# A fused convolution and attention layer: weights loaded from ScalarE's queue, and background work given out by estimated time

## The chip, the core and the metric

The kernel runs on one core of a Trainium2 chip. The time is the device time of one execution in microseconds (us); lower is better. TensorE (PE) multiplies matrices into PSUM, VectorE (DVE), ScalarE (ACT) and GpSimd (POOL) do elementwise work, and SyncE (SP) only issues transfers (DMA) here. Each engine runs its instructions in order and waits on semaphores where one needs another's result.

## The reference

One layer over 2048 positions of width 2048, in float32, cut to its core:

```python
proj = x @ w_in + b_in                                   # 2048 x 5376
c_val, c_glu, c_gate, q, k, v, a_gate = split(proj)
h = c_val * sigmoid(c_glu)                               # 1024 channels
h = causal_depthwise_conv(h, conv_w, 31 taps) + conv_b
y_conv = silu(layer_norm(h)) * silu(c_gate)
# 16 query heads of 64, 2 key/value heads, window 128, a learned sink per head
y_attn = window_attention(q, k, v, sinks) * silu(a_gate)
y = concat(y_conv, y_attn) @ w_out + b_out
out = layer_norm(2 ** 0.25 * x + y)
```

## The kernel before

**Three products for one.** To keep float32 accuracy each operand is split into a high part (rounded to the matmul format `fp32r`, a ScalarE copy, L135) and a low part, the rest (a subtraction, `lo_part`, L138, on VectorE or POOL). `mm3` (L795 to L797) then makes three matmuls of 128x512: high x high, low x high, high x low.

**Steps.** The program is written out as a list of 432 steps, each one weight tile of 128x1024 and 24 matmuls. The first 208 belong to the input projection: four chunks of 512 positions with 52 steps each. In a chunk, 8 steps `first` make four output tiles (k, v and the first convolution pair) side by side, 36 steps `in` make 18 tiles one after the other, and 8 steps `last` make four tiles side by side again. Then come 112 steps `gate` and 112 steps `out`, which use a Strassen scheme: two blocks with seven products each, of sums of weight quarters (`T`, `O` are those sums and their low parts, made by `tsum_part` on POOL and put aside in memory) and of sums of inputs (`gen_y`). Attention blocks (`att_scores`, `att_transpose`, `att_values`, three steps apart) are placed at steps 13 to 41 of each chunk.

**Weights.** At step n the program loads the weight tile of step n+3 (`load_w`), loads the stored low part of step n+2 (`load_lo`) where there is one, and splits step n+2 (`split_w`): a ScalarE copy, and a POOL subtraction where no low part is stored. Low parts of chunk 0 are stored (`wlo`) and loaded again in chunks 1 to 3. There are three buffers each of raw tile, high part and low part, so the load of a low part waits until TensorE has finished step n-1.

**Transfers.** `dma` (L75 to L77) issues everything from SP, in the order of the program: weights, inputs, intermediate results, stores. A transfer that waits for its source or its buffer holds all behind it. `store_later` puts a store a few steps behind the work that makes its source.

**Background work.** VectorE's convolution (31 taps for each 128 channels and chunk, L234 and L237) and the normalizations wait in a queue `tq` and a generator `convs`; `run_bg(n)` takes n items at the end of each step: 4 or 5 in the input steps, 3 or 4 in gate, 1 or 2 in out. Within an engine, the build orders instructions by the program's order and its own simulated readiness.

**The end.** The last four steps run row block by row block, each followed by its normalization (`tail_norm`) and stores; their weights are loaded by `tail_w` into other buffers.

Of the kernel before, what the change touches and what calls it, by code (L numbers as in the profile page):

```python
# [16 lines left out]
P = 128  # L17
# [13 lines left out]
NSLOT = 69  # L31

# [16 lines left out]

@with_exitstack  # L50
def hybrid_layer_kernel(ctx, tc, x, xT, w_first, w_in, w_out, consts, b_out, ln_g, ln_b, out):
    nc = tc.nc
    V, A, G, T = nc.vector, nc.scalar, nc.gpsimd, nc.tensor
# [17 lines left out]
    def dma(out, in_):  # L71

        if queue:
            with tc.issue_after(queue.pop()):
                queue.append(nc.sync.dma_start(out=out, in_=in_).ins)  # L75
        else:
            queue.append(nc.sync.dma_start(out=out, in_=in_).ins)  # L77

# [301 lines left out]
    def evac_in(c, t, kind, j, ps):  # L380
# [11 lines left out]
        elif kind == "k":  # L392
            for t in (*ks, *kl):
                copy(t[:, 0:P], t[:, 4 * P:5 * P].bitcast(F32))
# [15 lines left out]
        elif kind == "v":  # L410
            raw = slot(f"vraw{c}")
            A.activation(out=raw, in_=ps, func=AF.Identity, bias=b1)
            copy(vt[:, 0], vt[:, 4].bitcast(F32))
# [160 lines left out]
    wlo = [dram.tile([P, 1024], F32, tag=f"wlo{n}", name=f"wlo{n}") for n in range(52)]  # L574
# [70 lines left out]
    def out_norm(c):  # L645
# [9 lines left out]
        def fin(n):  # L655
            def f():
                if n + 2 < 16:
                    d, s = units[n + 2]
                    load_z(c, s, d)
                if n < 16:  # L660
                    d, s = units[n]
                    if s == 0 and d < 3:
                        load_gb(c, d + 1)
                    norm_unit(c, s, d)
                if n >= 4:
                    d, s = units[n - 4]
                    store(c, s, d)
            return f
        return [first] + [fin(n) for n in range(20)]
# [35 lines left out]
    def load_w(n, parts=1):  # L705
# [171 lines left out]

    w0 = load_w(0, 2)
# [16 lines left out]
    for n, s in enumerate(steps):  # L895
# [24 lines left out]
        if n < PER:  # L920
# [3 lines left out]
        if s[0] in ("first", "last"):  # L924
# [15 lines left out]
            if p == 7 and s[0] == "first":  # L940
                for t in (2, 3, 1, 0):
# [4 lines left out]
            run_bg(5)  # L946
        elif s[0] == "in":
# [10 lines left out]
            run_bg(4 if 13 <= n % PER < 42 else 5)  # L958
        elif s[0] == "gate":
# [11 lines left out]
            run_bg(3 + n % 2)  # L971
        else:
# [28 lines left out]
            run_bg(2 if blk == 1 and (i == 4 or i == 7 and n % 2) or len(tq) > 20 else 1)  # L1001
# [6 lines left out]
            if n == len(steps) - 1:  # L1008
                run_bg(len(tq))
                tail_banks()  # L1010
                for tp in range(4):
# [3 lines left out]
                    tail_norm(3, tp)  # L1015
        if n < TAIL:
# [9 lines left out]
    run_bg(len(tq))  # L1026
# [67 lines left out]
```

## Time and profile before

| | |
|---|---|
| median of 3 runs | 2646.96 us (2645.77 to 2650.88) |
| the profiled execution | 2649.56 us, span 2647.8 us |
| busy: PE, DVE, ACT, POOL | 96%, 78%, 50%, 38% |
| moved by DMA | 720.43 MB, mean 272 GB/s |
| granted TensorE clock, mean | 0.989 |

The span runs from the first to the last instruction. Engine shares are busy time by span; SP's issues aren't counted as busy. In the rows shown below, a group is written as line, engine, operation, written tile <- read tiles, with its count; a wait as "who <- for whom: us in total, times, longest".

### The profile page before, as it was taken

Reading aid. Unit: us, or ns where it says so; the run is one execution under the profiler, and the core shown is the slowest. Engines: PE = TensorE matmul, PEld = TensorE weight load, DVE = VectorE, ACT = ScalarE, POOL = GpSimd, SP = SyncE. Lnnn points to the kernel's source line nnn. Section 1 sums busy time; section 2 is a strip of 40 time slices with the busy share of each in tenths; the row PEclk is TensorE's granted clock in tenths of the full one; section 3 lists DMA queues with packets and bytes.
Section 4 is the critical chain, followed back from the end, with each engine's and each line's share of the span. In section 5 each row is a group of like instructions: output and inputs, shape, how many; then the busy total and the mean of one; then the engine's idle time right before and its main releaser. Section 6 shows DMA issues by size and latency. Waiting matters only on the chain.

```text
span 2647.8 us, 35533 instructions
## 1 busy us (share of the span) xinstructions
PE 2547.2 (96%) x11680; PEld 2107.5 (80%) x11680; DVE 2069.5 (78%) x3215; ACT 1328.5 (50%) x2520; POOL 1006.3 (38%) x636
## 2 busy tenths in 40 slices
PE   8999999999899999999999999999999999999986
PEld 7788877877688887888887787888888888888875
DVE  3787798868888858889759899987775677987676
ACT  4677335776347765467536434544554323333244
POOL 2777824455144451426423222324222222222246
PEclk9999999999999999999999999999999999999998
DMA  8675898757987689866887667786888987899876
GB/s 282 218 259 198 285 330 272 244 176 267 343 297 246 202 304 348 319 227 224 270 277 250 238 232 270 272 285 217 287 287 289 331 299 281 285 347 351 277 255 244
DMA packets 331674, 720.43 MB, mean 272 GB/s; under 512 B 37856, under 2 KB 95328, under 8 KB 331488
## 3 DMA queue, kind: packets, MB, share of 16 engines
q1 hardware_dynamic: 331488, 718.16, 78.3%
q8 instruction: 92, 1.51, 0.2%
q14 instruction: 94, 0.77, 0.1%
HBM read 564.79 MB, written 153.21 MB: 271 GB/s over the span
## 4 chain that ended last, share of the span: by engine, by line
PE 52%; DVE 22%; DMA 10%; ACT 7%; issue 4%; SPq 2%; POOL 2%; DVEq 0%; ACTq 0%; POOLq 0%
DVE cv L237 7%; PE in L797 4%; PE in L795 4%; PE in L796 4%; PE out L796 3%; PE out L797 3%; PE out L795 3%; SPq L75 2%; PE out_s L796 2%; PE out_s L797 2%; PE out_s L795 2%; PE gate_s L797 1%; PE gate_s L795 1%; PE gate_s L796 1%; ACT pr L325 1%
## 5 line engine op out<-in xcount | busy, mean ns | idle before, releaser
L138 POOL TENSOR_TENSOR wl<-wr,wh 128x1024 fp32r<-128x1024 f32 (+1 forms) x158 | 397.9, 2520 | 938.8 <-ACT wh L135 679.1
L135 ACT ACTIVATE wh<-wr 128x1024 fp32r<-128x1024 f32 (+1 forms) x436 | 455.1, 1046 | 529.1 <-DMA wr<-in_w_in_dram 68.6
L237 DVE SCALAR_TENSOR_TENSOR cv<-h,cst,cv 128x512 f32<-128x512 f32 x928 | 696.4, 752 | 18.8
L795 PE MATMUL in<-xh,wh 128*128 128x512 f32 x1280 | 503.7, 394 | 10.1 <-ACT xh L135 5.8
L797 PE MATMUL in<-xh,wl 128*128 128x512 f32 x1280 | 501.4, 393 | 11.3 <-DMA wl<-wlo 11.2
L796 PE MATMUL in<-xl,wh 128*128 128x512 f32 x1280 | 501.7, 392 | 0.0
L797 PEld LDWEIGHTS in<-xh,wl 128*128 128x128 f32 x1280 | 241.9, 189 | 65.3 <-DMA wl<-wlo 15.3
L795 PEld LDWEIGHTS in<-xh,wh 128*128 128x128 f32 x1280 | 242.2, 189 | 59.9 <-ACT xh L135 6.6
L796 PEld LDWEIGHTS in<-xl,wh 128*128 128x128 f32 x1280 | 242.0, 189 | 48.7 <-DVE xl L138 1.0
L135 ACT ACTIVATE yhout<-yrout 128x512 fp32r<-128x512 f32 x112 | 70.0, 627 | 223.8 <-DVE yrout L560 206.2
L796 PE MATMUL out<-wl,yhout 128*128 128x512 f32 x448 | 174.9, 390 | 5.9 <-POOL wl L138 5.9
L797 PE MATMUL out<-wh,ylout 128*128 128x512 f32 x448 | 174.4, 389 | 0.0
L138 POOL TENSOR_TENSOR plc<-pmc,phc 128x512 fp32r<-128x512 f32 x64 | 83.1, 1299 | 222.4 <-ACT phc L135 194.7
L795 PE MATMUL out<-wh,yhout 128*128 128x512 f32 x448 | 166.5, 389 | 0.0
L138 DVE TENSOR_TENSOR ylgate<-yrgate,yhgate 128x512 fp32r<-128x512 f32 x112 | 110.9, 991 | 42.4 <-ACT yhgate L135 41.1
L138 DVE TENSOR_TENSOR ylout<-yrout,yhout 128x512 fp32r<-128x512 f32 x112 | 103.4, 925 | 50.7 <-ACT yhout L135 49.4
L325 ACT ACTIVATE pr<-pr,sm 128x128 f32<-128x128 f32 x256 | 99.6, 390 | 68.7 <-DVE sm L321 68.3
L135 ACT ACTIVATE yhgate<-yrgate 128x512 fp32r<-128x512 f32 x112 | 69.9, 624 | 114.8 <-DVE yrgate L560 94.3
L795 PE MATMUL gate_s<-yhgate,wh 128*128 128x512 f32 x304 | 118.8, 391 | 2.8 <-DVE g L454 2.6
L797 PE MATMUL gate_s<-yhgate,wl 128*128 128x512 f32 x304 | 118.7, 390 | 2.5 <-POOL wl L138 1.9
L796 PE MATMUL gate_s<-ylgate,wh 128*128 128x512 f32 x304 | 118.3, 389 | 0.0
L795 PE MATMUL gate<-yhgate,wh 128*128 128x512 f32 x288 | 112.7, 391 | 0.2 <-DVE g L454 0.2
(383 smaller groups left out, 5914.3 us busy)
## 6 DMA issues: line engine op xcount, KB each, us to landing
wl<-wlo SPq DMA_DIRECT2D x156, 512.0 KB, 5.3
wr<-in_w_in_dram SPq DMA_DIRECT2D x144, 512.0 KB, 5.9
yrout<-yd SPq DMA_DIRECT2D x192, 256.0 KB, 5.8
wr<-in_w_in_dram SPq DMA_DIRECT2D x320, 128.0 KB, 4.3
yrgate<-in_xT_dram SPq DMA_DIRECT2D x144, 256.0 KB, 4.9
wr<-T_gate SPq DMA_DIRECT2D x64, 512.0 KB, 6.3
wr<-T_out SPq DMA_DIRECT2D x61, 512.0 KB, 7.2
wl<-O_gate SPq DMA_DIRECT2D x56, 512.0 KB, 3.9
```

The costliest lines, as they stand in the source:

```text
L75: queue.append(nc.sync.dma_start(out=out, in_=in_).ins)
L135: A.activation(out=dst, in_=src, func=AF.Copy)
L138: eng.tensor_tensor(out=dst, in0=src, in1=hi.bitcast(F32), op=ALU.subtract)
L237: V.scalar_tensor_tensor(out=a if t == TAPS - 1 else acc, in0=x_, scalar=w, in1=acc, op0=ALU.mult, op1=ALU.add)
L325: A.activation(out=p3[:, u, :], in_=p3[:, u, :], func=AF.Exp, scale=HD ** -0.5, bias=sm[:, 1, u:u + 1], accum_out=sm[:, 3, u:u + 1])
L795: T.matmul(o, lh, mh, start=start, stop=False)
L796: T.matmul(o, lh, ml, start=False, stop=False)
L797: T.matmul(o, ll, mh, start=False, stop=stop)
```

## The change

- `T.matmul`s on a zeroed tile: ten of 128x512 into a PSUM bank, ahead of the first load.
- `wdma`: like `dma`, but issued by ScalarE and chained to one another there. Raw weight tiles from step 8 on and all stored low parts go that way; `tail_w` keeps SP.
- Low parts are no longer stored and loaded for `first` and `last`: POOL subtracts in these steps (VectorE in steps 0 to 7, as before). `wlo` shrinks from 52 tiles to the 36 of the `in` steps.
- `Metered` wraps VectorE and adds up an estimate of each operation's time. `run_bg()` without a number adds (5.44 + a share for each attention part of the step) x 0.865 us to what may be spent, carries over at most 1 us, and takes items until what VectorE was given since the last step exceeds it. It is called once at the end of each step but the last.
- Stores: the normalized convolution 5 steps behind (3 before), the normalized output 4 steps behind its unit (in place of 4 units). What is pending is issued ahead of the tail.
- The five copies that carry keys and values over from the last chunk stand at step 4 of a chunk, and its first four tiles are evacuated in the order k, v, cval, cglu (before: cval, cglu, v, k).

```diff
+WARM = 10
+STEP, SHARE = 5.44, 0.865
+BESIDE = {"att_scores": 2.0, "att_transpose": 0.4, "att_values": 1.0}
...
+class Metered:
+    def __getattr__(self, op):
+        f = getattr(self.engine, op)
+        def call(**kw):
+            t = kw["in_"] if op in ("tensor_reduce", "bn_stats", "bn_aggr") else kw["out"]
+            n = 1
+            for d in t.shape[1:]:
+                n *= d
+            self.us += 0.16 + n / 960 + (0.06 if op == "scalar_tensor_tensor" else 0.0)
+            return f(**kw)
+        return call
...
-    V, A, G, T = nc.vector, nc.scalar, nc.gpsimd, nc.tensor
+    V, A, G, T = Metered(nc.vector), nc.scalar, nc.gpsimd, nc.tensor
...
+    def wdma(out, in_):
+        if wqueue:
+            with tc.issue_after(wqueue.pop()):
+                wqueue.append(nc.scalar.dma_start(out=out, in_=in_).ins)
+        else:
+            wqueue.append(nc.scalar.dma_start(out=out, in_=in_).ins)
...
-    def run_bg(n):
-        for _ in range(n):
+    def run_bg(n=None):
+        if n is None:
+            us = STEP + sum(BESIDE.get(f.__name__, 0.0) for f, *_ in att.get(st["n"], []))
+            st["spare"] = min(st.get("spare", 0.0), 1.0) + us * SHARE
+        while n or n is None:
+            was = V.us
+            if n is None and was - st.get("seen", 0.0) > st["spare"]:
+                break
             if tq:
                 tq.popleft()()
             else:
                 next(convs)
+                if n is None and V.us == was:
+                    break
+            n = n and n - 1
+        if n is None:
+            st["spare"] -= V.us - st.get("seen", 0.0)
+            st["seen"] = V.us
...
-                store_later(od[c, 8 + j], u, 3)
+                store_later(od[c, 8 + j], u, 5)
...
-                if n >= 4:
-                    d, s = units[n - 4]
-                    store(c, s, d)
+                    later.append((st["n"] + 4, lambda: store(c, s, d)))
...
-                dma(out=t[:, w], in_=src[:, w] if parts > 1 else src)
+                (dma if n < 8 else wdma)(out=t[:, w], in_=src[:, w] if parts > 1 else src)
...
     def has_lo(n):
-        return n >= PER and (steps[n][0] not in strassen or steps[n][4] % 2 == 0)
+        kind = steps[n][0]
+        return n >= PER if kind == "in" else kind in strassen and steps[n][4] % 2 == 0
...
-            dma(out=t.bitcast(F32), in_=lo_src(n))
+            wdma(out=t.bitcast(F32), in_=lo_src(n))
...
-                lo_part(G if steps[n][0] != "first" else V, lo[:, w], t[:, w], hi[:, w])
+                lo_part(V if n < 8 else G, lo[:, w], t[:, w], hi[:, w])
...
+    warm = slot("warm", F32R)
+    nc.vector.memset(warm.bitcast(F32), 0.0)
+    wps = right_banks("warm")[3]
+    for k in range(WARM):
+        T.matmul(wps, warm[:, 0:P], warm, start=k == 0, stop=k == WARM - 1)
...
-        if n < PER:
+        if n in wlo:
             dma(out=wlo[n], in_=los[n].bitcast(F32))
...
-                for t in (2, 3, 1, 0):
+                for t in range(4):
                     evac_in(c, t, *ORDER[t], st["acc"][t])
...
-            run_bg(5)
+            if p == 4 and s[0] == "first":
+                for t in (*ks, *kl):
+                    copy(t[:, 0:P], t[:, 4 * P:5 * P].bitcast(F32))
+                copy(vt[:, 0], vt[:, 4].bitcast(F32))
...
             if n == len(steps) - 1:
                 run_bg(len(tq))
+                for _, f in later:
+                    f()
+                later.clear()
                 tail_banks()
...
+        if n < len(steps) - 1:
+            run_bg()
```

More of the change, by code (lines that the diff above doesn't have):

```diff
@@ L47, in col_tiles, with __init__ @@
     return order
+class Metered:
+    def __init__(self, engine):
+        self.engine, self.us = engine, 0.0
+    def __getattr__(self, op):
[8 more added lines that the diff above has]
+        return call
 @with_exitstack
@@ L392, in evac_in @@
         elif kind == "k":
-            for t in (*ks, *kl):
-                copy(t[:, 0:P], t[:, 4 * P:5 * P].bitcast(F32))
             for kv in range(2):
@@ L412, in evac_in @@
             A.activation(out=raw, in_=ps, func=AF.Identity, bias=b1)
-            copy(vt[:, 0], vt[:, 4].bitcast(F32))
             pt = ps_pt.tile([P, 4, P], F32, tag="pt", name=f"vT{c}")
@@ L573, in hybrid_layer_kernel @@
            for i in range(1, 8) for q in pieces if q[2] % 2 == 0}
-    wlo = [dram.tile([P, 1024], F32, tag=f"wlo{n}", name=f"wlo{n}") for n in range(52)]
+    wlo = {n: dram.tile([P, 1024], F32, tag=f"wlo{n}", name=f"wlo{n}") for n in range(8, 44)}
     def quarter(what, dp, p, a, b):
@@ L664, in f @@
                     norm_unit(c, s, d)
-                if n >= 4:
-                    d, s = units[n - 4]
-                    store(c, s, d)
+                    later.append((st["n"] + 4, lambda: store(c, s, d)))
             return f
-        return [first] + [fin(n) for n in range(20)]
+        return [first] + [fin(n) for n in range(16)]
     PER = 52
@@ L1025, in hybrid_layer_kernel @@
                     yc.pop((s[0], blk, i, 2 * p + kk))
-    run_bg(len(tq))
     for _, f in later:
```

4 lines of the change are left out of this document (1 added, 3 removed).

## The prediction

> **What bounds the kernel now.** I read the page's head first, then the busy time by stretch (stretches cut at step bounds), then TensorE's waits, then those of the transfer queue.
>
> ```profile
> span 2647.8 us, 35533 instructions
> PE 2547.2 (96%) x11680; PEld 2107.5 (80%) x11680; DVE 2069.5 (78%) x3215; ACT 1328.5 (50%) x2520; POOL 1006.3 (38%) x636
> q1 hardware_dynamic: 331488, 718.16, 78.3%
> ```
>
> TensorE is the bound, and all transfers run in one queue, at 78.3%. But 96% is not the distance to the floor, since matmuls overlap. The stretches tell it (columns: length, busy of PE, PEld, DVE, ACT, POOL with counts, granted clock, DMA share, GB/s):
>
> ```profile
> 0.00:85.00 85.00, 77.11 (x324) 62.26 (x325) 33.23 (x46) 37.98 (x54) 23.46 (x32) 0.98 0.80 267
> 85.00:302.70 217.70, 208.24 (x1059) 176.42 (x1058) 164.81 (x293) 142.95 (x368) 171.67 (x109) 0.99 0.70 236
> 302.70:432.30 129.60, 120.50 (x518) 97.43 (x517) 114.56 (x154) 48.84 (x66) 55.27 (x36) 0.97 0.88 300
> 432.30:656.50 224.20, 211.96 (x1063) 178.27 (x1062) 177.15 (x340) 159.45 (x393) 109.35 (x82) 0.98 0.70 235
> 656.50:784.20 127.70, 119.66 (x517) 96.35 (x516) 103.26 (x142) 51.06 (x69) 39.24 (x31) 0.99 0.92 325
> 784.20:994.20 210.00, 207.20 (x1060) 175.69 (x1059) 161.69 (x321) 144.10 (x370) 101.46 (x80) 1.00 0.73 251
> 994.20:1118.60 124.40, 120.09 (x519) 98.05 (x519) 107.47 (x157) 60.92 (x86) 42.45 (x33) 0.97 0.94 333
> 1118.60:1329.20 210.60, 206.93 (x1058) 175.24 (x1057) 172.14 (x334) 138.10 (x354) 90.39 (x70) 1.00 0.71 246
> 1373.30:1739.60 366.30, 355.19 (x1540) 289.38 (x1539) 336.65 (x457) 171.46 (x241) 105.86 (x44) 0.99 0.73 253
> 1739.60:2004.50 264.90, 262.68 (x1157) 216.82 (x1156) 193.74 (x248) 137.98 (x192) 72.74 (x33) 1.00 0.77 272
> 2004.50:2352.70 348.20, 348.20 (x1538) 288.26 (x1537) 257.77 (x371) 111.83 (x146) 82.24 (x32) 1.00 0.86 301
> 2352.70:2577.80 225.10, 219.22 (x962) 179.81 (x961) 167.23 (x231) 75.68 (x97) 66.86 (x31) 1.00 0.86 306
> 2577.80:2611.80 34.00, 24.29 (x98) 19.32 (x97) 25.42 (x39) 8.85 (x12) 22.85 (x10) 0.85 1.01 344
> 2611.80:2647.80 36.00, 21.83 (x97) 17.75 (x95) 23.43 (x52) 22.53 (x55) 18.80 (x15) 0.84 0.38 145
> ```
>
> From 2004.5 to 2352.7 TensorE is never idle: 348.2 / 1538 = 0.2264 us for each 512-wide matmul, so a step of 24 takes 5.43 us. With it I find what each stretch loses. The start (0 to 85): 85 - 325 x 0.2264 = 11.4. The three chunk changes (last tiles of one chunk, first of the next, and the five steps behind): 129.6 - 117.3 = 12.3, 127.7 - 117.0 = 10.7, 124.4 - 117.5 = 6.9, together 29.9. The attention stretches have the same matmuls in each chunk, so they are compared with each other: 217.7, 224.2, 210.0, 210.6; the first two lose 7.7 and 14.2 against the third. Gate: 366.3 - 348.7 = 17.6 and 264.9 - 261.9 = 3.0. Output: 0, then 225.1 - 217.8 = 7.3 and 34.0 - 22.2 = 11.8. These 103 us and a little inside chunks 2 and 3 are all that can be had; the last 36 us hold 22 of matmuls and the final normalization, which isn't touched.
>
> Who is waited for:
>
> ```profile
> PE in L797 <- DMA wl<-wlo: 11.2, 7, 3.5
> PE pv L361 <- DVE ya L372: 10.4, 6, 3.4
> PE out_s L796 <- DMA wl<-O_out: 8.9, 1, 8.9
> PE sc L310 <- DVE pr L318: 8.6, 10, 1.4
> PE out L796 <- POOL wl L138: 5.9, 5, 3.1
> PE in1l_s L797 <- DMA wl<-wlo: 5.7, 3, 3.3
> PE pt L338 <- DVE pmu L343: 5.3, 6, 2.8
> PE gate_t L795 <- ACT wh L135: 4.1, 3, 2.0
> ```
>
> Two families: the loads of low parts (at the chunk changes, where the DMA share is 0.88 to 0.94, and at the end), and VectorE in the attention. Behind several of these stalls the granted clock of the stretch falls (0.97, 0.98, 0.85), so a stall costs more than its length. The queue's own waits say why loads are late:
>
> ```profile
> SPq L75 <- POOL wl L138: 120.8, 35, 11.8
> SPq L75 <- DVE gu L165: 75.1, 20, 12.6
> ...
> SPq L75 <- DVE ylout L138: 9.7, 1, 9.7
> ```
>
> A store or a load that waits for VectorE holds every weight behind it. The last row is from 2560 to 2600, beside the 8.9 us stall.
>
> **Low parts by POOL in `first` and `last`.** This drops 16 of the 52 stores and 48 of the 156 loads below, 64 x 0.5 MB, of which 48 transfers fall into the three changes; it adds 48 subtractions on POOL. The rows: those transfers, the copy ahead of a subtraction, and the subtraction.
>
> ```profile
> wl<-wlo SPq DMA_DIRECT2D x156, 512.0 KB, 5.3
> wlo<-wl SPq DMA_DIRECT2D x52, 512.0 KB, 5.6
> ...
> L135 ACT ACTIVATE wh<-wr 128x1024 fp32r<-128x1024 f32 (+1 forms) x436 | 455.1, 1046 | 529.1 <-DMA wr<-in_w_in_dram 68.6
> ...
> L138 POOL TENSOR_TENSOR wl<-wr,wh x158: 1302/2402/7659, 42.8 to 2607.9; 128x1024 fp32r<-128x1024 f32 x154, 128x512 fp32r<-128x512 f32 x4
> ```
>
> In a change, 16 transfers are 8 MB of 129.6 us x 300 GB/s = 39 MB, a fifth. The waits on `wlo` there (11.2 + 5.7 us) lose their object. POOL takes 8 or 16 x 2.4 = 19 or 38 us more where it is busy 55, 39 and 42 of about 127 us. The copy and the subtraction take 1.05 + 2.4 us of the two steps, 10.9 us, between a buffer's release and its use; even the slowest subtraction, 7.7, fits behind a copy. I keep 8 of the 29.9 us: **gain 22** (10 if POOL queues behind its other sums, 28 if all goes).
>
> **Weights issued by ScalarE.** Counts and durations of one issue (ns, smallest, median, largest):
>
> ```profile
> L75 SPq DMA_DIRECT2D wr<-in_w_in_dram x464: 327/428/1636, 31.4 to 1895.1; - x155
> L75 SPq DMA_DIRECT2D wl<-wlo x156: 319/320/1618, 346.2 to 1358.6; - x156
> ```
>
> By the code about 880 issues move: those 464, 24 first tiles, 61 and 64 summed quarters, 48 output quarters, 108 `wlo`, 56 and 55 sums' low parts. At 0.32 to 0.43 us, about 340 us on ScalarE, 50% to 63% busy. The trace has no issue on ScalarE. Its price on the path lies between 0 (hidden in ScalarE's idle time) and 340. In the attention a step adds 0.75 us, 23 in 31 steps: 182 of 224.2, 167 of 210.0, 161 of 210.6. That is nearer to hidden; I take **7 us lost**. Behind a waiting issue on ScalarE stand copies of `wh`, the exponentials and PSUM evacuations. The low part's load waits for the buffer that step n-1 of TensorE frees, but the `wh` copy next to it waits for that step as well, so ScalarE is held little longer than today. Freed of the 120.8, 75.1 and 9.7 us waits above, the weights in the gate and output stages arrive on time: of 17.6 + 3.0 I keep 9, **gain 11**; of 7.3 + 11.8 I keep 8, **gain 11** (0 to 17 each). What is late next there is VectorE: 25.4 us busy in that stretch of 34, where TensorE has 22 of work.
>
> **Meter.** Each step gets (5.44 + what attention adds) x 0.865 us of VectorE work, foreground included, in place of 3 to 5 items.
>
> ```profile
> L237 DVE SCALAR_TENSOR_TENSOR cv<-h,cst,cv 128x512 f32<-128x512 f32 x928 | 696.4, 752 | 18.8
> L138 DVE TENSOR_TENSOR ylgate<-yrgate,yhgate 128x512 fp32r<-128x512 f32 x112 | 110.9, 991 | 42.4 <-ACT yhgate L135 41.1
> ```
>
> A tap is metered at 0.16 + 512/960 + 0.06 = 0.753 us, as measured. Five taps are 3.8 us; the foreground of an attention step comes on top, hence the rows `ya`, `pr`, `pmu` (24.3 us of waits). With the meter the first two chunks should come near the other two: 211 each, all four 844 for 862.5, **gain 18** (0 if ScalarE's added 10% takes VectorE's place, 30 if chunks 2 and 3 gain too). The total fits: 432 x 4.71 + 64 x 3.4 x 0.865 = 2223 us for 2069.5.
>
> **The rest.** Stores that are issued two steps later (and those of the normalized output four steps behind their unit) take the DVE waits off the transfer queue; counted above. The order of the evacuations and the five early copies shorten the hand-over to step 8 by about 1 us. The zero matmuls act on this:
>
> ```profile
> 10.60 0.63 PE L797 MATMUL in<-xh,wl 128*128 128x512 f32 x1
> 11.02 0.43 PE L795 MATMUL in<-xh,wh 128*128 128x512 f32 x1
> 11.29 0.40 PE L796 MATMUL in<-xl,wh 128*128 128x512 f32 x1
> 11.53 0.39 PE L797 MATMUL in<-xh,wl 128*128 128x512 f32 x1
> ```
>
> Until 11.0 matmuls start 0.43 us apart, then 0.23. Ten at 0.43 fill the 4.3 us ahead of the first real one. Some ten real ones are then 0.2 us shorter, of which the third tile's late weights take part back: with the hand-over **gain 2.5** (0 to 4). The Trainium skill ("TensorE: Matmul & The Clock Gate", Part 1) says that the array runs at half clock until about 3.4 us of activity have passed, in a free-running window; the spacing of the rows agrees, and by the page the zero matmuls would cover it wholly, which changes the sum by less than 1 us.
>
> **Sum.** 22 - 7 + 11 + 11 + 18 + 2.5 = 57.5 us off the profiled execution's own 2649.56 (span 2647.8 and 1.8 around it): 2592. The median of the runs, 2646.96, lies 2.6 lower: **2589**.
>
> **The rivals.** *The queue brings nothing* (0.20). All transfers use the same 16 engines, at 0.86 to 1.01 in the output stage; a second queue then only reorders. Then gate and output gain 0 and the changes about 15 from the bytes: 15 - 7 + 18 + 2.5 = 28.5, 2618. For it speaks the 0.86; against it the SP rows, which are waits before the issue. The Trainium skill ("DMA: Bandwidth & Descriptors", section "Issuing engines are not separate DMA queues") says just this, that several issuers save only the time to start a transfer; it would leave the queue's waits as they are counted here.
>
> *The meter misses* (0.10). It counts a 512-wide subtraction at 0.69 us, the row shows 0.99, so VectorE is really loaded nearer to 0.95, and what the meter holds back piles up in the gate stage or ahead of the tail (17 normalization units). Attention and gate then gain nothing: 57.5 - 29 = 28.5, 2618 too; with 17 x 0.69 = 12 us of leftover, 2630.
>
> *Slower: ScalarE comes late with the low parts* (0.08). Some 219 of these loads are now issued when ScalarE's turn comes. From the buffer's release there are 10.9 us, less 0.32 for the issue and 5.3 for the landing: 5.2 us for ScalarE's backlog, and on an attention step of 224.2 / 31 = 7 us it would be busy 182 / 31 = 5.9. At 0.42 us of stall per load, 92 us: 2681. It decides from 57.5 / 219 = 0.26 us per load. Against it: the `wh` copies have the same place in line today and stop TensorE for only 4.1 us.
>
> *It does little* (0.07): the build orders the engines by its own simulated times, so that ScalarE's issues may come no sooner than SP's did: 2640 to 2652.
>
> **Numbers.** The forecast has 0.55, with 2552 to 2615 as its own range (the terms' upper ends in part together: 28 + 30 + 17 + 17 + 4 = 96; lower ends in part, 32). To hold 8 in 10 the range goes to the two rivals near 2618 to 2630: 2552 to 2632. A difference of 0.2%, 5 us, is what a measurement can tell here. Faster: 0.55 + 0.20 + 0.10 + 0.03 = 0.88; same 0.04; slower 0.08.
>
> **What would show it.** Right: no wait of TensorE on `wlo` at the chunk changes and a DMA share there below 0.8; attention stretches within 2 us of each other, with fewer than 10 us of waits on `ya`, `pr` and `pmu`; no 8.9 us stall near 2580; a second hardware queue with well over half the bytes; ScalarE's share of busy time not much changed, with its idle time shorter. Wrong: rows `PE in L797 <- DMA wl<-wlo` inside the attention stretches, new TensorE waits for ACT, or VectorE busy without a break ahead of the gate's end.

## The result, and the profile after

The changed kernel took 2742.19 us (median of 4 runs, 2739.79 to 2754.28), the kernel before 2647.36 us beside it: 1.0365 times as long, 95% interval 1.0333 to 1.0398. That is 95 us slower, where 57.5 us of gain were forecast and the range ended at 2632. The profiled execution has a span of 2742.0 us.

The page's head and its queues, after:

```profile
span 2742.0 us, 35378 instructions
PE 2583.8 (94%) x11690; PEld 2132.8 (78%) x11690; DVE 2114.1 (77%) x3216; ACT 1324.6 (48%) x2520; POOL 1113.6 (41%) x684
q1 hardware_dynamic: 195552, 349.00, 37.0%
q10 hardware_dynamic: 126720, 335.60, 36.5%
```

There are now two hardware queues of about equal bytes, and the engines' busy times are much what they were: no other engine took TensorE's place as the busiest. The busy time by stretch, after, cut at the same steps as before (the last two rows are the gate stage, here in halves; columns as in the prediction):

```profile
81.30:316.00 234.70, 215.09 (x1059) 180.87 (x1058) 175.17 (x302) 142.35 (x366) 169.53 (x107) 0.96 0.63 216
316.00:457.90 141.90, 124.02 (x515) 100.10 (x514) 120.71 (x163) 47.41 (x66) 77.18 (x47) 0.94 0.65 219
457.90:701.50 243.60, 223.28 (x1064) 185.11 (x1063) 184.28 (x342) 159.58 (x390) 112.06 (x84) 0.93 0.64 218
701.50:829.80 128.30, 118.55 (x518) 97.18 (x517) 108.86 (x149) 51.35 (x75) 77.79 (x48) 0.96 0.79 266
829.80:1060.60 230.80, 213.23 (x1062) 178.79 (x1061) 167.65 (x321) 145.16 (x371) 106.23 (x80) 0.97 0.66 220
1191.30:1411.80 220.50, 211.75 (x1061) 178.01 (x1060) 180.45 (x341) 139.51 (x356) 95.66 (x73) 0.98 0.68 232
1465.10:1777.70 312.60, 308.26 (x1344) 253.17 (x1345) 283.50 (x381) 143.38 (x197) 76.99 (x32) 0.99 0.77 258
1777.70:2089.30 311.60, 308.24 (x1350) 254.01 (x1349) 212.32 (x283) 156.16 (x220) 85.42 (x38) 0.99 0.80 266
```

The gate stage begins at 1465.1 (before: 1373.3), so 92 us, the whole loss, lie in the input stage. The attention stretches went from 217.7, 224.2, 210.0, 210.6 to 234.7, 243.6, 230.8, 220.5, the first chunk change from 129.6 to 141.9. Gate takes 624.2 in place of 631.2, output 652.7 in place of 643.3. The DMA share fell in all of these input stretches (0.70 to 0.63 in the first attention) and rose a little in gate: the engines of the transfers are not what is short. All rows of TensorE's waits together come to 86.5 us before and 140.8 after, and by the mean granted clock (0.989 and 0.973) TensorE lost 0.011 x 2648 = 29 and 0.027 x 2742 = 74 us of full speed. As an estimate, 54 us more of waits and 45 of clock, 99 together, cover the loss of 94 in the span. The longest of TensorE's waits, after:

```profile
PE pv L406 <- DVE ya L69: 13.0, 8, 3.3
PE out_s L839 <- DVE ylout L69: 12.1, 4, 6.9
PE pt L383 <- DVE pmu L69: 11.1, 3, 5.3
PE in0l_s L839 <- POOL wl L170: 10.2, 2, 5.6
PE in L837 <- ACT gt L432: 9.4, 3, 6.4
PE in_s L837 <- ACT gt L432: 8.9, 2, 8.5
```

Of the waits on `wlo` that the change aimed at (11.2 + 5.7 us), 1.2 us is left. By what they wait for, TensorE's waits on DMA fell from 26.4 to 9.8 us; those on ACT rose from 14.8 to 50.5, on DVE from 34.0 to 59.7, on POOL from 11.3 to 20.8. The 8.5 us wait, seen from ScalarE (timeline, after: start, duration, instruction, idle time ahead of it and what ended it):

```profile
754.20 0.33 ACTq L107 DMA_DIRECT2D wr<-in_w_first_dram  x1
754.63 1.15 ACT L167 ACTIVATE xh<-xr 128x512 fp32r<-128x512 f32 x2 [3.23 <-POOL wl L170]
755.69 1.04 ACT L167 ACTIVATE wh<-wr 128x1024 fp32r<-128x1024 f32 x1
756.63 0.67 ACT L429 ACTIVATE gu<-in1l_s,half 128x512 f32<-128x512 f32 x1
757.20 0.68 ACT L432 ACTIVATE gt<-in1l_s,half 128x512 f32<-128x512 f32 x1
```

from POOL:

```profile
751.48 2.69 POOL L170 TENSOR_TENSOR wl<-wr,wh 128x1024 fp32r<-128x1024 f32 x1 [1.89 <-ACT wh L167]
```

and from TensorE:

```profile
757.93 0.79 PE L837 MATMUL in_s<-xh,wh 128*128 128x512 f32 x1 [8.47 <-ACT gt L432]
```

The issue of a raw weight tile at 754.20 writes a buffer that POOL reads until 754.17. ScalarE stands for 3.23 us ahead of it; the evacuations `gu` and `gt` of finished PSUM tiles are queued behind, and TensorE needs those banks for `in_s`. That is a part of the 8.47 us. Just before, ScalarE had also been idle for 5.74 and 1.75 us until input tiles `xr` landed, which SP issues; the second cause, below, bears on those.

ScalarE's standing is its idle time from the end of its last instruction to the start of such an issue. Over the trace it adds up to 383 us: 173 in 73 waits of `wr` for a POOL subtraction, 136 at low parts' issues that wait for TensorE to free their buffer, 71 until another transfer has landed. 220 us of the 383 are in the input stage.

SP, which should have become free, waits as well. Its waits, before:

```profile
SPq L75 <- DMA wr<-T_out: 20.1, 27, 1.8
SPq L75 <- DMA wr<-in_w_in_dram: 12.6, 20, 1.7
```

and after:

```profile
SPq L98 <- DMA wr<-in_w_in_dram: 459.5, 137, 18.1
SPq L98 <- DVE gu L69: 164.1, 20, 27.9
SPq L98 <- DMA wr<-T_out: 133.1, 39, 14.5
SPq L98 <- DMA wl<-O_out: 131.6, 31, 7.6
```

SP, which issues only stores, inputs and intermediate results now, waits for *weight transfers*, up to 18 us at a time: 1205 us in all such rows, 103 before. The built program shows why. These are five issues of SP that follow one another (four stores and a low part's load, in the kernel of the seventh experiment below), with the semaphores that each waits for:

```
zd_0_1_23106<-xn_0_1_22482 128x512 [waits DMAHW3_49,DVE_49]
zd_1_1_23109<-xn_1_1_22536 128x512 [waits DMAHW4_49,DVE_49]
zd_2_1_23112<-xn_2_1_22577 128x512 [waits DMAHW5_49,DVE_49]
zd_3_1_23115<-xn_3_1_22621 128x512 [waits DMAHW6_49,DVE_49]
wl_23168<-O_out_0_375 128x1024 [waits DMAHW7_49,PE_49,Pool_49]
```

The build gives transfers eight completion semaphores, 0 to 7, in turn, whichever engine issues them, and an issue waits until the transfer that had the same semaphore last has landed. In this program all 2302 transfers take them strictly in turn, and in the trace of the changed kernel 1348 of SP's 1358 issues wait for the very semaphore that they will update. (The Trainium skill, "DMA: Bandwidth & Descriptors", section "Why a DMA increments its semaphore by 16 and not by 1", gives a reason: with two transfers in flight on one semaphore, the count can be reached before the first has landed. No run here shows such a case.) In the single queue of before, the transfer eight places ahead has nearly always landed: SP's waits for weights are at most 2.8 us long. With two queues it is often one that the other engine issued late.

### The profile page after: what moved, and what is told of

It is laid out like the page before. It is cut to its first block, busy times and chain, and to the rows that moved or that the text cites. A ratio compares the mean times of both kernels' runs of the same rounds, so it can differ in the third digit from the quotient of the medians.

```text
span 2742.0 us, 35378 instructions
## 1 busy us (share of the span) xinstructions
PE 2583.8 (94%) x11690; PEld 2132.8 (78%) x11690; DVE 2114.1 (77%) x3216; ACT 1324.6 (48%) x2520; POOL 1113.6 (41%) x684
## 4 chain that ended last, share of the span: by engine, by line
PE 44%; DVE 18%; DMA 12%; ACT 6%; issue 4%; POOL 3%; ACTq 1%; SPq 0%; DVEq 0%; POOLq 0%
DVE cv L69 6%; PE in L839 4%; PE in L837 4%; PE in L838 4%; PE out L838 2%; PE out L837 2%; PE out L839 2%; DVE xn L69 2%; DMA wr<-in_w_in_dram 2%; PE gate_s L837 2%; PE gate_s L839 2%; PE gate_s L838 2%; PE gate L837 2%; PE gate L839 2%; PE gate L838 2%
## 5 line engine op out<-in xcount | busy, mean ns | idle before, releaser
L170 POOL TENSOR_TENSOR wl<-wr,wh 128x1024 fp32r<-128x1024 f32 (+1 forms) x206 | 508.6, 2470 | 1079.4 <-ACT wh L167 752.4
L69 DVE SCALAR_TENSOR_TENSOR cv<-h,cst,cv 128x512 f32<-128x512 f32 x928 | 687.6, 751 | 17.3
L837 PE MATMUL in<-xh,wh 128*128 128x512 f32 x1280 | 513.2, 401 | 29.1 <-ACT gt L432 9.4
L839 PE MATMUL in<-xh,wl 128*128 128x512 f32 x1280 | 510.2, 399 | 7.9 <-POOL wl L170 6.2
L838 PE MATMUL in<-xl,wh 128*128 128x512 f32 x1280 | 510.4, 399 | 0.0
L837 PE MATMUL out<-wh,yhout 128*128 128x512 f32 x448 | 174.2, 389 | 0.0
L69 DVE TENSOR_TENSOR ylout<-yrout,yhout 128x512 fp32r<-128x512 f32 x112 | 110.2, 986 | 50.3 <-ACT yhout L167 49.4
L839 PE MATMUL gate<-yhgate,wl 128*128 128x512 f32 x288 | 112.7, 392 | 0.8 <-DMA wl<-O_gate 0.8
```

Source lines behind the costliest of these rows:

```text
L69: return f(**kw)
L170: eng.tensor_tensor(out=dst, in0=src, in1=hi.bitcast(F32), op=ALU.subtract)
L837: T.matmul(o, lh, mh, start=start, stop=False)
L838: T.matmul(o, lh, ml, start=False, stop=False)
L839: T.matmul(o, ll, mh, start=False, stop=stop)
```

## The experiments

Each is compared with the kernel before on the same chip; a difference is between the two medians there. Those that start from the changed kernel come first.

**1. The parts of the queue.** All weights back to SP; only raw tiles back to SP; only low parts back to SP:

```diff
# all on SP: both lines; raw on SP: the first; low parts on SP: the second
-                (dma if n < 8 else wdma)(out=t[:, w], in_=src[:, w] if parts > 1 else src)
+                dma(out=t[:, w], in_=src[:, w] if parts > 1 else src)
...
-            wdma(out=t.bitcast(F32), in_=lo_src(n))
+            dma(out=t.bitcast(F32), in_=lo_src(n))
```

> The changed kernel with all weights issued by SP again, the rest of the change kept. Theory A (ScalarE is held: the load of a raw tile stands at the head of ScalarE's order and waits there for POOL's subtraction, which frees the buffer, while copies, exponentials and PSUM evacuations wait behind it): the loss of 95 us and more goes, 2590 to 2640. Theory B (the meter: it gives VectorE, and by it ScalarE, background work in bursts ahead of what TensorE waits for): stays above 2700. Theory C (POOL's added subtractions in the first and last steps come late): stays above 2700.

> The changed kernel with only the raw tiles issued by SP again; the stored low parts stay with ScalarE. Theory A, if it is the wait for POOL that matters: within 25 us of the run with all weights on SP. If it is any issue on ScalarE, or the low parts' wait for TensorE: less than half of that run's gain. Theories B and C: stays above 2700.

> The changed kernel with only the stored low parts issued by SP again, the raw tiles stay with ScalarE. Theory A1: little gain, 2715 to 2740, since the raw tiles' waits stay. Theory A2 by the number of issues (220 of 880): 19 of the 77 us, 2723. If the two parts of the queue add up: 77 - 28 = 49 us, 2693.

Measured: all on SP 2665.28 (1.0072, 1.0055 to 1.0088); raw on SP 2713.89 (1.0257, 1.024 to 1.0275); low parts on SP 2775.77 (1.0486, 1.0464 to 1.0507). Without the queue, 77 of the 95 us are gone, and SP's waits for weight transfers are 87 us. The 2665 lie above the range that was expected for it. Either half of the queue alone costs: 49 us with only low parts on ScalarE, where ScalarE stands 145 us (98 of them for TensorE, 35 for POOL) and SP waits 788 us for weight transfers; 111 us with only raw tiles there (435 and 926 us), more than both halves together, which no expectation had. Standing and SP's waits change together in these runs, so they don't tell the two apart; experiments 7 and 8 do.

**2. The meter and the low parts, undone.** Fixed counts of items instead of `run_bg()`; low parts stored and loaded in `first` and `last` as before:

```diff
         if n < len(steps) - 1:
-            run_bg()
+            run_bg(5)    # shortened: 5 in first and last, 4 or 5 in, 3 or 4 gate, 1 or 2 out, as before
```

```diff
-        kind = steps[n][0]
-        return n >= PER if kind == "in" else kind in strassen and steps[n][4] % 2 == 0
+        return n >= PER and (steps[n][0] not in strassen or steps[n][4] % 2 == 0)
...     # and wlo has all 52 tiles again
```

> The changed kernel with the fixed numbers of background items of the kernel before, the rest of the change kept. Theory A: no gain, 2725 to 2760. Theory B: 2660 or less. Theory C: no gain.

> The changed kernel with the low parts of the first and last steps stored and loaded again (all 52, by ScalarE's queue), so POOL subtracts there no more. Theory A: a part, since fewer buffers are then freed by POOL: 2690 to 2730. Theory B: no gain. Theory C: 2660 or less.

Measured: fixed counts 2745.75 (1.0368, 1.0353 to 1.0383), stored low parts 2725.86 (1.03, 1.0285 to 1.0315). Under the queue the meter is worth nothing either way, and POOL's low parts cost 16 us.

**3. A fourth raw buffer,** so that the load needn't wait for POOL:

```diff
-NSLOT = 69
+NSLOT = 67
...
-    wraw = ctx.enter_context(tc.tile_pool(name="wraw", bufs=3))
+    wraw = ctx.enter_context(tc.tile_pool(name="wraw", bufs=4))
```

> The changed kernel with four raw weight buffers in place of three (and 67 slots in place of 69, for room), so that the load at the head of ScalarE's order waits for the subtraction of one step earlier. Theory A1 (what costs is ScalarE standing still at a raw tile's load until POOL has freed the buffer; the trace of the changed kernel has 175 us of such idle time): 2690 to 2715, about the 28 us that came back with the raw tiles on SP. Theory A2 (what costs is the place of the issues in ScalarE's fixed order, whatever they wait for): no gain, 2725 to 2755.

Measured: 2744.65 (1.0364, 1.0345 to 1.0383), no gain, and ScalarE still stands 365 us, 163 of them for POOL (173 with three buffers). So the edit didn't take the standing away, and the run speaks neither for nor against it. A likely reason, not shown, is that the build places a load where its own simulation first sees a free buffer, so that with four buffers the issue moved forward.

**4. Each part alone on the kernel before:** the queue; the meter; POOL's low parts; and all the rest (zero matmuls, later stores, order of the evacuations, early copies), each by the lines that the change has for it.

> The kernel before with nothing but the weights' transfers moved to ScalarE. Both theories of the queue: slower, by 77 us if it doesn't need the rest of the change (2725), by 30 to 50 if the waits for POOL's added subtractions are part of it (2677 to 2697). My forecast's reading (loads freed from SP's order): 2625 or less.

> The kernel before with nothing but the meter. From undoing it in the changed kernel (no difference in all, the gate stage 31 us longer without it, the input stage shorter): gate stage 20 to 30 us shorter, input stage as much longer, 2637 to 2657. My forecast's reading: attention 18 us shorter, 2620.

> The kernel before with nothing but the low parts of the first and last steps made by POOL. My forecast: 22 us less, 2625. From the changed kernel, which gained 16 us when they were stored again: 2650 to 2665.

> The kernel before with the zero matmuls, the later stores, the order of the evacuations and the early copies alone. The start 4 to 6 us shorter (with all on SP it was 80 us to step 13, for 85), the rest unchanged: 2640 to 2646. If the parts add up to the change's 95 us (86 for the queue, 22 for the meter), this and the run on POOL's low parts are together 13 us faster.

| part alone | median, us | difference | ratio, 95% interval | prediction |
|---|---|---|---|---|
| queue | 2733.67 | +86 | 1.0339 (1.0313 to 1.0366) | -15 |
| meter | 2669.82 | +22 | 1.0097 (1.0078 to 1.0116) | -18 |
| POOL's low parts | 2664.89 | +16 | 1.0068 (1.005 to 1.0086) | -22 |
| the rest | 2641.28 | -8 | 0.9981 (0.9964 to 0.9997) | -2.5 |

They add up to +117, and together they cost 95. What POOL's low parts do, in TensorE's waits of that run:

```profile
PE in L798 <- POOL wl L138: 19.0, 8, 7.4
PE pv L361 <- DVE ya L372: 9.8, 5, 3.4
PE out_s L797 <- DMA wl<-O_out: 8.5, 1, 8.5
PE in L796 <- ACT wh L135: 8.3, 2, 6.1
```

and in the stretch of the last chunk change, which took 124.4 us before:

```profile
987.50:1137.10 149.60, 125.84 (x520) 100.27 (x519) 129.76 (x157) 60.28 (x86) 87.90 (x50) 0.91 0.66 224
```

The waits on `wlo` are gone, and waits on a chain of two engines have come: a low part now needs ScalarE's `wh` first and then 2.5 us of POOL. Nearly the whole loss lies in this one change, 25 us; the first change took 123.9 us (129.6 before), the second 127.8 (127.7). In the wait of 7.4 us POOL runs through nine other operations, from 1086.0 to 1097.4, ahead of the subtraction; a wait of 6.1 us for `wh` goes back to a raw tile that SP issued late, behind a store that stood 9.5 us for VectorE's `gu`. The 520 matmuls are 117.7 us of work in 149.6, and the clock of the stretch is 0.91. The DMA share is down from 0.94 to 0.66, as forecast, and nothing is won by it.

**5. Issues behind the copy.** Kernel before with the queue, but each ScalarE load is chained behind the step's own `wh` copy (the low part's load moves into `split_w`, behind that copy):

```diff
+    def wdma(out, in_):
+        with tc.issue_after(held[-1]):   # the step's wh copy
...
+            split_w(n + 2)
             list(load_w(n + 3))
-            load_lo(n + 2)
-            split_w(n + 2)
```

> The kernel before with the weights on ScalarE, as in the run with the queue alone (2734), but each load put behind the copy of the same step's tile in ScalarE's order, where its buffer is free or nearly so. Theory A1: most of the 86 us come back, 2640 to 2680, and ScalarE's idle time at loads that wait for POOL or TensorE falls from 273 us to under 80. Theory A2: no gain, above 2710. If the loads then land too late: waits of TensorE's matmuls on wl and of the copies on wr, in place of the others.

Measured: 2946.32 (1.114, 1.1096 to 1.1184). ScalarE stands only 23 us, and chunk 0's attention takes 221 us (236 with the queue alone, 218 before); but a new bound came with the edit. A load can start only behind the copy of the tile before, and the next copy needs it: 0.33 us for the issue, 5.6 to 6.3 for the landing, 1.06 for the copy are 7 us or more against a step of 5.43, and the last output steps take 350 / 52 = 6.7 us. So for the whole time this run shows nothing on the standing.

**6. Tiny transfers.** Kernel before with 928 extra ScalarE transfers of one column each (128x4 bytes), meant as the price of an issue:

```diff
+        with tc.issue_after(held[-1]):
+            dq.append(nc.scalar.dma_start(out=d, in_=ident[:, 0:1]).ins)
```

> The kernel before, its weights on SP, with one added transfer on ScalarE beside each weight transfer from step 8 on (about 880 of 128 x 4 bytes, from a constant to a place of its own, so none of them waits for anything), each behind the copy of its weight tile. It shows what the issues cost by themselves. Theory A1 (ScalarE standing still in issues that wait): 2645 to 2665. Theory A2 (the time and place of the issues): 2700 or more; 880 x 0.33 us would be up to 290.

Measured: 5278.01, 1.9946 times (1.9875 to 2.0018). 928 issues of 0.33 us don't cost that. SP's first row of waits says where the time goes:

```profile
SPq L75 <- DMA dm<-ident: 2379.5, 462, 17.6
```

SP stood behind them for 2.4 ms, by the shared semaphores. But this isn't a measure of the coupling alone. The tiny transfers themselves took long, about 12.9 us in the median from issue to landing, and all others became slow beside them: `wl<-wlo` lands after about 12.0 us in place of 5.3, and the packets of SP's queue took 83.8% of 5260 us for the same 718 MB that took 78.3% of 2648 before. In the other runs with two queues that packet time hardly moved (76.8% of 2729 us with the queue alone).

**7. A second queue without standing, and its control.** Raw tiles on ScalarE behind the step's copy (chained as in 5), but for tile n+4 into four buffers (as in 3), so that the buffer is free when ScalarE comes; low parts on SP. The control has the same order and buffers, with everything on SP.

```diff
             load_lo(n + 2)
             split_w(n + 2)
-            list(load_w(n + 3))
+            list(load_w(n + 4))
...
-                dma(out=t[:, w], in_=src[:, w] if parts > 1 else src)
+                (dma if n < 8 else wdma)(out=t[:, w], in_=src[:, w] if parts > 1 else src)   # not in the control
```

> Kernel before, raw weight tiles from step 8 on issued by ScalarE, but each behind that step's own rounding copy, for the tile of step n+4 with four raw buffers (two slots of the pool fewer), so that the buffer has been free for a step or more when ScalarE comes to the issue and ScalarE need not stand; stored low parts stay in SP's queue. Theory 1 (the loss of the queue is ScalarE standing at issues whose buffer POOL still reads): 2650, at most 2660, and chunk 0's attention stretch at 222 or less (236 with the queue alone). Theory 2 (the loss is that the two queues share their completion semaphores, so that SP waits for ScalarE's transfers): SP's waits for weight transfers stay above 600 us and the time is above 2690.

> Control to the run above: the same order (tile n+4 behind the step's copy, four raw buffers), all issued by SP. Both theories: 2647 within 10 us, SP's waits for weight transfers about 100 us. If it is itself above 2670, the run above is compared with this one and not with the kernel before.

Measured: 2751.44 (1.0393, 1.0373 to 1.0414), the control 2667.55 (1.0072, 1.0057 to 1.0087; twice as far from before as the expectation allowed: 7 us in chunk 0's attention and 13 in gate, why isn't traced). ScalarE stands 36 us, chunk 0's attention takes 224 us in the one and 225 in the other, and yet the second queue costs 84 us. SP's waits with the queue:

```profile
SPq L75 <- DMA wr<-in_w_in_dram: 293.9, 103, 8.9
SPq L75 <- DMA wr<-T_gate: 133.7, 32, 8.2
SPq L75 <- DMA wr<-T_out: 116.6, 35, 7.6
```

and in the control:

```profile
SPq L75 <- DMA wr<-in_w_in_dram: 23.3, 29, 1.5
SPq L75 <- DMA wr<-T_out: 23.8, 30, 2.4
```

All of SP's waits for weight transfers are 788 and 125 us. One of them in SP's timeline, with the queue:

```profile
2474.37 1.27 SPq L75 DMA_DIRECT2D yrout<-yd  x3
2480.11 0.34 SPq L75 DMA_DIRECT2D out_dram<-xn  x1
2480.50 2.88 SPq L75 DMA_DIRECT2D zd<-xn  x4
2483.48 0.70 SPq L75 DMA_DIRECT2D wl<-O_out  x1
```

and where it ends in TensorE's:

```profile
2489.04 0.50 PE L807 MATMUL out_s<-wl,yhout 128*128 128x512 f32 x1 [3.27 <-DMA wl<-O_out]
```

Up to 2480.11 SP waits 4.5 us for a `wr<-T_out` that ScalarE issued at 2475.46, in order to issue a *store* of a finished output, which has nothing to do with that weight. The low part behind the store is issued at 2483.48 and TensorE stands for it. The low parts also take longer once issued: in the median `wl<-O_out` 6.0 us in place of 4.1 in the control, `wl<-O_gate` 4.9 for 3.6, `wl<-wlo` 5.4 for 4.9; a raw tile of the other queue may be under way beside them, but that this is why isn't shown. In the output stage the two effects are about as large: the low parts are issued 2.6 us on average behind the step that frees their buffer (1.0 in the control) and land 5.9 us after that (4.6), and 12 of 54 land less than 0.5 us ahead of their step, in place of 2. TensorE's waits on DMA are 55.9 us here and 29.5 in the control, those on ACT 42.0 and 22.2.

**8. Standing without a second queue.** Kernel before, all on SP; ScalarE reads one column of POOL's low part at the place of the load, so that it waits as the issue did:

```diff
             list(load_w(n + 3))
+            if n in los and not has_lo(n):
+                tch = small.tile([P, 1], F32, tag="tch", name=f"tch{n}")
+                copy(tch, los[n][:, 0:1].bitcast(F32))
             load_lo(n + 2)
```

> Kernel before with every transfer left on SP; ScalarE copies one column (128x1) of the low part that POOL has made for tile n, at the place in the program where the raw tile n+3 is loaded, and so waits for the same subtraction as that issue would, with no transfer and no second queue. About 150 copies of some 0.2 us, 30 us of work for ScalarE. Theory 1 (standing): chunk 0's attention stretch, where POOL subtracts for every step, goes from 218 to 228 to 236, and the whole time to 2665 to 2690. Theory 2 (coupled queues): no stretch moves by over 3 us and the time is at most 2655.

Measured: 2676.22 (1.0104, 1.0089 to 1.0119), 30 us more. The copies' own group (the last column is the idle time ahead of them), and the stretches of the first two attentions:

```profile
L135 ACT ACTIVATE tch<-wl 128x1 f32<-128x1 f32 x154 | 31.1, 202 | 355.1 <-POOL wl L138 355.1
```

```profile
88.10:326.50 238.40, 216.34 (x1058) 182.22 (x1057) 168.47 (x294) 147.22 (x398) 172.38 (x110) 0.96 0.65 217
459.60:683.40 223.80, 212.19 (x1062) 178.02 (x1061) 177.41 (x340) 159.61 (x393) 108.85 (x82) 0.98 0.69 235
```

ScalarE stands 355 us, about as long as in the changed kernel, and chunk 0's attention, where POOL subtracts in every step, takes 238.4 (217.7 before), as it does with the queue alone (236). Of the 355 us, 39 lie in that stretch, with the queue alone 43. Another 280 lie in gate and output, which get 2 us longer together: standing costs by its place, not by its length. In the attentions of chunks 1 to 3 low parts are loaded and this run has no such copy (223.8 in chunk 1, 224.2 before); but there the queue alone stands for only 7 to 10 us each and loses 19, 12 and 8. So standing explains chunk 0's attention and perhaps a part of the first chunk change, 20 to 30 of the queue's 86 us, and not the rest.

**9. The time of the issues.** The control of 7 with one more ScalarE copy of 128x160 for each raw transfer:

```diff
                 dma(out=t[:, w], in_=src[:, w] if parts > 1 else src)
+                if n >= 8:
+                    held()     # copy(busy, cst[:, 0:160]), chained behind the step's wh copy
```

> The control with tile n+4 and four raw buffers, every transfer issued by SP, and behind each step's rounding copy one more ScalarE copy of 128x160 for each raw transfer of the step (some 660 in all, about 0.33 us each, as long as the row of an issue on ScalarE). So ScalarE has the time of the issues and nothing of the queue. Theory 1b (what is left of the queue's loss once ScalarE stands no more is the time of the issues on ScalarE): 2735 to 2760, as with these loads on ScalarE (2751). Theory 2 (it is the coupling of the two queues): 2665 to 2685.

Measured: 2662.85 (1.0063, 1.0042 to 1.0084); the control was 2667.55. The 661 copies took 215.6 us of ScalarE (326 ns each) and cost nothing, so what the queue of 7 loses against its control is not the time of the issues. By these runs what is left is the coupling of the queues: SP's waits for the other queue's transfers, and low parts that land later. No run takes one of the two away alone; kernels with separate semaphores weren't tried.

**10. The meter.** The meter alone without the extra time at attention's steps, which gives every step 5.44 x 0.97 = 5.28 us; and the rest's kernel (2641) with the meter in the gate stage only, 5.44 x 0.92 = 5.0 us a step (shortened):

```diff
-STEP, SHARE = 5.44, 0.865
-BESIDE = {"att_scores": 2.0, "att_transpose": 0.4, "att_values": 1.0}
+STEP, SHARE = 5.44, 0.97
+BESIDE = {}
```

```diff
             if hf == 1:
                 evac_in(c, t, kind, j, ps)
             run_bg(4 if 13 <= n % PER < 42 else 5)
...
-            run_bg(3 + n % 2)
+            run_bg()     # gate only, SHARE 0.92
```

> Kernel before with the meter alone, but without the extra time at attention's steps: 5.44 x 0.97 = 5.28 us for each step, the operations' counted times unchanged. Theory M (the meter costs because it lets most background into the steps that have the most of attention's own work, whose subtractions take longer than it counts): the attention stretches of chunks 1 and 2 come back from 235 and 225 to within 3 us of 224 and 210, the whole time to 2645 to 2657. Rival (it is the order of the items, whatever their number): 2665 or more, the two stretches within 4 us of 235 and 225.

> Kernel before with the small parts (zero matmuls, later stores, order of evacuation, early copies) and the meter in the gate stage alone, at 5.44 x 0.92 us for each step; 4 or 5 items in the input steps and 1 or 2 in output as before. The small parts alone were 2641. If the meter's gain in the gate stage (321 to 311 us with the meter alone) is its own and not what the attention lost before it: 2628 to 2636. Rival (gate was shorter because input stages left other work): 2638 to 2655.

Measured: 2688.86 (1.0163, 1.0146 to 1.018) and 2659.99 (1.0044, 1.003 to 1.0057). Attention of chunks 1 and 2, then the gate's first half, with the meter alone:

```profile
433.10:668.40 235.30, 215.23 (x1063) 180.57 (x1062) 186.39 (x348) 160.03 (x393) 113.16 (x85) 0.96 0.67 231
1396.90:1707.80 310.90, 307.42 (x1345) 253.07 (x1344) 280.44 (x379) 145.80 (x201) 78.46 (x33) 0.99 0.77 263
```

and without the extra time:

```profile
432.30:655.30 223.00, 211.51 (x1062) 178.14 (x1061) 147.85 (x286) 159.61 (x393) 114.04 (x85) 0.98 0.70 241
1378.10:1712.90 334.80, 314.06 (x1349) 255.16 (x1348) 307.79 (x411) 153.58 (x214) 86.52 (x39) 0.98 0.71 245
```

Chunk 1's attention came back from 235.3 to 223.0 and chunk 2's from 225 to 210, as expected; but the gate's first half went from 310.9 to 334.8, with VectorE busy 92% of it, and the total got worse. The meter moves VectorE's work between two stages that both stall for it: what it takes from the one is due in the other. The second run agrees: with the earlier stages' work unchanged, the first half of the metered gate took 330 us and not 311 (323 with fixed counts, the rest alone), so the gate's gain was not the meter's own. Both runs also allowed a gate step more than the change did (4.7 us), and that wasn't separated. Why the work is dearer metered than in fixed counts isn't settled. One part of it stands in the trace of before: VectorE's 512-wide subtraction `ylgate` takes the metered 0.69 us in the 81 cases without a POOL instruction beside it, and 1.78 us on average in the 31 with one.

No run beats the rest alone: 2641.28 us, faster than both kernels, by a ratio whose interval (0.9964 to 0.9997) just leaves out 1.

## Why the prediction was wrong

**The queue: "7 us lost", "gain 11" and "gain 11".** The step that failed is "ScalarE is held little longer than today". It looked at low parts alone, whose buffer and whose `wh` copy wait for the same step of TensorE. The raw loads wait for something else, POOL's subtraction, and this stood in the prediction's own row (120.8 us, 35 times, on SP). It counted that row as a gain: freed of it, weights arrive on time. But a wait at an in-order issue isn't removed by another queue; it moves to the engine that issues, and ScalarE, unlike SP, has the rest of the kernel behind it. Experiment 8 puts this at 20 to 30 us. The second cause is one that no row of before pointed at: the two queues aren't independent. Experiment 7 has it at 84 us in its own arrangement; in the queue alone it is what is left by subtraction, some 55 to 65. The two runs don't add up to 86, so how the loss divides is an estimate. The 7 us for the time of the issues was right or even too much (experiment 9). Of the two gains, gate won 7 us and output lost 9 in the changed kernel; with the queue alone, gate lost 16.

**Low parts by POOL: "gain 22".** Measured alone: 16 us lost. The aim was hit: TensorE's waits on `wlo` at the changes vanished and the DMA share there fell from 0.88-0.94 to 0.65-0.79 in the changed kernel. The step that failed is "even the slowest subtraction, 7.7, fits behind a copy" into 10.9 us: it took copy and subtraction as starting when the buffer is released. In the last change `wh` came late once, since SP had issued its raw tile late, and once POOL's subtraction stood behind nine other operations, so that the chain was late by up to 7.4 us. A load has no such chain. The prediction's own "10 if POOL queues behind its other sums" had the mechanism and not the size; that it hit one change of three, and gained 6 us in another, can be an accident of the order.

**Meter: "gain 18".** Measured alone: 22 lost. "With the meter the first two chunks should come near the other two" was wrong in sign: chunks 1 and 2 went to 235 and 225. The step took the row `cv` (0.753 us, as metered) for the whole, and set the rest aside as a rival with 0.10. That rival's place was right (attention and gate), its size not: it let both gain nothing, where the attentions of chunks 1 and 2 lost 26 us and gate won 8.

**The rest: "gain 2.5".** The sign was right and the term too small: 8 us alone (interval 1 to 10). The start took 79.8 us in place of 85.0, so the zero matmuls and what stands beside them are worth some 5.

**The rivals.** "Slower: ScalarE comes late with the low parts", 2681, had the right engine and sign, and by luck: it had TensorE wait for late low parts, and those waits on DMA fell to 9.8 us in all. The measured standing is mostly at raw tiles, and most of it cost nothing (355 us of it cost 30). The rival by the rule of the Trainium skill ("DMA: Bandwidth & Descriptors", section "Issuing engines are not separate DMA queues") has two halves here. That several issuers bring no more transfer agrees with the runs: with the queue alone the same 720 MB moved at a mean of 264 GB/s, 272 before. That the time to start a transfer is all there is to the choice doesn't: that time was worth nothing, and the choice cost 86 us.

**What would show it.** Two of the signs of "right" came true (no waits on `wlo` at the changes, a DMA share below 0.8) in a kernel that was 95 us slower; the sign of "wrong" that decided was the new waits for ACT. A sign that only says that the intended wait is gone doesn't say that the time is.

## What to carry to other kernels

Before an issue is moved to a compute engine, list what each such transfer waits for (the buffer's last reader above all) and what is queued behind the issue on that engine; the wait moves with it. A second queue isn't independent if the build hands completion semaphores round: look at what each issue waits for in the built program, and at the old queue's waits in the first profile after. When a transfer is replaced by computing, price the chain of engines that the result now needs, at the busiest moment, not the added instructions.

## What the runs showed of the hardware that was not expected

- ScalarE's standing is cheap where something else covers it: 355 us cost 30 us, 21 of them in the one attention stretch where POOL subtracts in every step, while 280 us of it in gate and output cost 2; 216 us of added copies cost nothing.
- 928 transfers of 0.5 KB doubled the time (1.99): they took about 12.9 us to land in the median, the 512 KB low parts beside them about 12.0 in place of 5.3, and SP waited 2379.5 us for 462 of the tiny ones.
- VectorE's 512-wide subtraction takes 0.69 us without a POOL instruction beside it and 1.78 us on average with one (81 and 31 cases of `ylgate`, before).
- A stall costs more than its length: between before and after TensorE's waits grew by 54 us and the clock took another 45 (0.989 to 0.973); with the queue alone 56 and 20 (0.982). Behind the 8.47 us wait at 757.93 the matmuls start 0.43 us apart, in the stretch without idle time 0.23. That low clock follows idle time agrees with the Trainium skill ("TensorE: Matmul & The Clock Gate", Part 1).
